# Attention weights left undivided, and the reciprocal of their sum applied to the attention output

## The chip, the core and the metric

The kernel runs on one core of a Trainium2 chip. The metric is device time in microseconds of one execution of the whole program, as the median of several runs; lower is better. Single rows come from one profiled execution, whose times are counted from its first instruction.

## The reference, cut to what matters

The program is one layer of a hybrid decoder: a sliding-window attention group and a state-space group side by side on 2064 tokens of a prompt (and 32 tokens of samples), an output projection, and a squared-ReLU MLP. The change touches the attention of the prompt only:

```python
def sink_softmax(logits, mask, sink):
    logits = jnp.where(mask, logits, NEG)
    m = jnp.maximum(jnp.max(logits, axis=-1, keepdims=True), sink)
    e = jnp.exp(logits - m)
    return e / (jnp.sum(e, axis=-1, keepdims=True) + jnp.exp(sink - m))

p = sink_softmax(logits, mask, sink)          # 8 heads, 2 key/value heads, window 128
o = jnp.einsum('bnkgqs,bnskd->bnqkgd', p, v)  # the output of a query is linear in its weights p
```

All arithmetic is float32. A product of two float32 tiles is made of three TensorE products of their high and low parts (helper `mm3`, L108; helper `split`, L93: ScalarE writes the rounded high part, and VectorE or GpSimd the difference).

## The kernel before

The program has four stages: a projection for the state-space input (`phase_u`), a loop over 16 tiles of 128 queries that carries attention and state space together (`phase_att`), the gated unit and output projection (`phase_mix`), and the MLP (`phase_mlp`). The order of instructions on each engine is fixed when the program is built: a planner walks the instructions in program order with its own estimate of when each is ready, so that neighbours in the code can be apart in a queue. Each engine then takes its queue strictly in order.

One turn of the loop at L993, for tile `i`:

- `scores` (L805): 24 products for two halves `u` (four heads each) into four banks of PSUM; VectorE adds the mask and takes the row maximum (L824); L827 forms minus the maximum of it and the sink; ScalarE makes the exponentials in `e` with their sums in `mx[:, u, 3]` (L830). L828 and L832 form the exponential of the sink's part in `mx[:, u, 2]`.
- `tr(i + 1)` (L781) turns the next tile's queries and keys; `qkv(i + 2)` (L431, L745) multiplies 48 products for the queries, keys and values of the tile after that, into two banks that `rope` reads.
- `rden` (L834): sum plus sink (L836), reciprocal (L837). `normal` (L839): the weights times the reciprocal, on VectorE for `u == 0` (L843, four instructions of 128x256) and on ScalarE for `u == 1` (L845, four).
- `ptrans` (L847): 16 transposes of `e` on TensorE (L852) into four banks, split by ScalarE into `PTh` and by VectorE into `PTl`.
- `rope(i + 2)` (L748): ScalarE takes queries, keys and values out of the two banks of `qkv` (L755, L754, L759); VectorE rotates them (L764 to L767) and reads the last of them at L768, which frees the second bank.
- `pv` (L858): 24 products of weights and values into one bank `po`; at the end of it ScalarE copies `po` into `at` with a change of column order (L871), and stores it in `ATD`.
- `split_x(i + 3)` (L735): ScalarE writes `axh`, GpSimd `axl` (L96).
- In between, one step of the state space (`s_split`, `s_in`, `s_rot`, `s_scan`, `s_hsplit`, `s_out`) and, on GpSimd, sums of MLP weights (L1476 to L1479).

Six banks of PSUM serve `scores`, `tr`, `qkv`, `ptrans` and `po` in turn (`mm_bank`, L75); a tile of the loop uses 13. Working tiles of 128x552 come from a pool of 25 (`t2`, L86), which the state space shares.

Of the kernel before, what the change touches and what calls it, by code (L numbers as in the profile page):

```python
# [58 lines left out]
def hymba_step(ctx: ExitStack, tc: tile.TileContext, A, O):  # L59
# [98 lines left out]

    # ------------------------------------------------------------------ u projection
    class Paced:  # L160
# [558 lines left out]
    def phase_att(outer, eq, qw, QP, X01):  # L719
        with ExitStack() as es:  # L720
# [6 lines left out]
            vr = [pw.tile([128, 4, 2, 192], F32R, name=f"v{n}") for n in range(2)]  # L727
            X, QK, QT, SM, PT, PO = {0: X01[0], 1: X01[1]}, {}, {}, {}, {}, {}

# [75 lines left out]
            def scores(i, u):  # L805
# [21 lines left out]
                DVE.scalar_tensor_tensor(mx[:, u, 1], mx[:, u, 0], -1.0, ng, op0=OP.mult, op1=OP.min)  # L827
                DVE.tensor_tensor(mx[:, u, 2], mx[:, u, 1], ng, op=OP.subtract)  # L828
                for j in range(4):
                    ACT.activation(e[:, u, j], e[:, u, j], AF.Exp, bias=mx[:, u, 1, j:j + 1],  # L830
                                   accum_out=mx[:, u, 3, j:j + 1])
                ACT.activation(mx[:, u, 2], mx[:, u, 2], AF.Exp)  # L832

            def rden(i, u):  # L834
                e, mx = SM[i]
                DVE.tensor_tensor(mx[:, u, 3], mx[:, u, 3], mx[:, u, 2], op=OP.add)  # L836
                DVE.reciprocal(mx[:, u, 3], mx[:, u, 3])  # L837

            def normal(i, u):  # L839
                e, mx = SM[i]  # L840
                for j in range(4):
                    if u == 0:
                        DVE.tensor_scalar(e[:, u, j], e[:, u, j], mx[:, u, 3, j:j + 1], None, op0=OP.mult)  # L843
                    else:
                        ACT.activation(e[:, u, j], e[:, u, j], AF.Copy, scale=mx[:, u, 3, j:j + 1])  # L845

# [11 lines left out]
            def pv(i, kv):  # L858
# [10 lines left out]
                if kv == 1:  # L869
                    at = wk.tile([128, 512], F32, name="at", tag="at", bufs=1)  # L870
                    ACT.activation(at.rearrange("p (k s c) -> p k c s", k=4, s=8),  # L871
                                   po.rearrange("p (k c s) -> p k c s", k=4, s=8), AF.Copy)
                    ACT.dma_start(ATD[:, :, :, 16 * i:16 * i + 16].rearrange("p k s c -> p (k s) c"),
                                  at.rearrange("p (a c) -> p a c", c=16))

            # state space: one pair of groups per step
            SX, SC, SS, SH = {}, {}, {}, {}
# [115 lines left out]
            for i in range(NT):  # L993
# [17 lines left out]
                for n, pr in enumerate(here):  # L1011
                    s_rot(pr)
                    if pr + 1 < NPR:
                        s_split(pr + 1)
                    if pr + 2 < NPR:
                        s_load(pr + 2)
                    if n == 0:
                        rden(i, 0)
                        normal(i, 0)
                        rden(i, 1)  # L1020
                        normal(i, 1)
                    s_scan(pr)
                    s_hsplit(pr)
                    if n == 0:
                        ptrans(i, 0)
                        if i + 2 < NT:
                            rope(i + 2)
                        ptrans(i, 1)
                    s_out(pr)
                    if pr + 1 < NPR:  # L1030
                        s_in(pr + 1)
                if not here:
                    for u in range(2):
                        rden(i, u)
                        normal(i, u)
                    ptrans(i, 0)
                    if i + 2 < NT:
                        rope(i + 2)
                    ptrans(i, 1)
                pv(i, 0)  # L1040
                if i + 3 < NT:
# [21 lines left out]

    # ------------------------------------------------------------------ gated unit, sample attention, output projection
    def advance(gen, n=1):
# [105 lines left out]
    def squares(pl, x, p, parts):  # L1171
        """sums of squares over the four channel tiles: [channel, token]"""
        q = pl.tile([128, 4, 128], F32, name="pq", tag="pq", bufs=1)
# [225 lines left out]

    # ------------------------------------------------------------------ MLP  # L1400
    # Both products are cut in halves along tokens, contraction and result (Strassen-Winograd): seven products
    # of quarters each, with the sums of the activations' quarters formed in place and those of the weights' once.
    HN = (336, 352, 352)
# [84 lines left out]
    def phase_mlp(pre):  # L1488
        with ExitStack() as es:
# [8 lines left out]
            def combine(p, n, pt, q, both):  # L1498
                """C11 = P1 + P2, C12 = P1 + P6 + P5 + P3, C21 = P1 + P6 + P7 - P4, C22 = P1 + P6 + P7 + P5"""
                if p == 1:  # L1500
# [47 lines left out]
            def rows(c, p):  # L1548
                """runs of up to 128 columns that hold tokens of one kind: (first column, number, rows of the output)"""
                out = []  # L1550
# [48 lines left out]
            def end_a(c, n):  # L1599
                """the first half of the features of the last tokens, scaled by the gain"""  # L1600
                f = M["H"].rearrange("p a c -> p (a c)")
# [171 lines left out]
```

## Time and profile before

| | us |
|---|---|
| median of 3 runs | 2208.49 |
| lowest and highest run | 2202.45, 2210.93 |
| the profiled execution, first to last instruction (its span) | 2198.8 |
| what the median has beside that span | 9.7 |
| the loop over 16 tiles, mean distance of its stages (from 211 to 564) | 23.6 |

The page gives no other time of the profiled execution than its span. Its first section has the busy time of each engine; the second cuts the span into 40 slices, with the share of each engine in tenths and the clock that TensorE was granted; the fourth follows the work that ended last back from the end. A group of instructions is shown with its line, engine, output and input, shape, count, busy time, mean duration, and the idle time of the engine in front of it with what ended that idle time. Matmuls overlap, and the ends of their rows are modelled, so that a duration there is longer than the distance to the next.

### The profile page before, as it was taken

Reading aid. Unit: us, or ns where it says so; the run is one execution under the profiler, and the core shown is the slowest. Engines: PE = TensorE matmul, PEld = TensorE weight load, DVE = VectorE, ACT = ScalarE, POOL = GpSimd, SP = SyncE. Lnnn points to the kernel's source line nnn. Section 1 sums busy time; section 2 is a strip of 40 time slices with the busy share of each in tenths; the row PEclk is TensorE's granted clock in tenths of the full one; section 3 lists DMA queues with packets and bytes.
Section 4 is the critical chain, followed back from the end, with each engine's and each line's share of the span. In section 5 each row is a group of like instructions: output and inputs, shape, how many; then the busy total and the mean of one; then the engine's idle time right before and its main releaser. Section 6 shows DMA issues by size and latency. Waiting matters only on the chain.

```text
span 2198.8 us, 37175 instructions
## 1 busy us (share of the span) xinstructions
PE 2083.1 (95%) x12968; PEld 1963.3 (89%) x12968; DVE 1645.6 (75%) x3412; ACT 1324.0 (60%) x2877; POOL 397.2 (18%) x435
## 2 busy tenths in 40 slices
PE   7888999997799999989999999999999999999997
PEld 7877888786678787889999999999999999999995
DVE  8947788788678647469896885787868757787686
ACT  6644655555665545537865555588555555875555
POOL 5513545455142334000000000000000000000001
PEclk9998999998899999999999999999999999999999
DMA  8894666655577526778745465454454564444554
GB/s 291 240 222 117 158 183 169 166 155 158 168 224 256 184 85 209 221 240 287 246 144 144 136 189 184 139 191 135 137 143 149 176 181 138 158 135 140 134 161 151
DMA packets 351972, 387.16 MB, mean 176 GB/s; under 512 B 96504, under 2 KB 239512, under 8 KB 351768
## 3 DMA queue, kind: packets, MB, share of 16 engines
q1 hardware_dynamic: 285096, 378.13, 56.9%
q10 hardware_dynamic: 65792, 4.20, 1.8%
q0 software_dynamic: 896, 2.46, 0.4%
q8 instruction: 101, 1.65, 0.3%
q14 instruction: 87, 0.71, 0.1%
HBM read 303.26 MB, written 82.46 MB: 175 GB/s over the span
## 4 chain that ended last, share of the span: by engine, by line
PE 70%; DVE 10%; DMA 9%; ACT 4%; issue 4%; POOL 1%; SPq 1%; POOLq 0%; DVEq 0%; ACTq 0%
PE mm L111 20%; PE mm L110 20%; PE mm L112 20%; PE mm L436 2%; PE mm L819 2%; DMA Y<-in_w_down_dram 2%; PE mm L437 1%; DMA wr<-TU 1%; DVE e L843 1%; DMA zu<-YD 1%; DMA wt<-in_w_down_dram 1%; DVE wsl L96 1%; DVE e L824 1%; DMA qwr<-in_w_in_dram 1%; ACT e L845 1%
## 5 line engine op out<-in xcount | busy, mean ns | idle before, releaser
L111 PE MATMUL mm<-vl,wsh 128*128 128x352 f32 (+1 forms) x2624 | 839.9, 320 | 0.0
L110 PE MATMUL mm<-vh,wsh 128*128 128x352 f32 (+1 forms) x2624 | 839.3, 321 | 0.1
L112 PE MATMUL mm<-vh,wsl 128*128 128x352 f32 (+1 forms) x2624 | 816.4, 321 | 12.1 <-DVE wsl L96 11.9
L95 ACT ACTIVATE wsh<-wr 128x512 fp32r<-128x512 f32 x684 | 430.3, 629 | 440.0 <-PE mm L111 425.5
L96 DVE TENSOR_TENSOR wsl<-wr,wsh 128x512 fp32r<-128x512 f32 x684 | 471.4, 691 | 178.4 <-ACT wsh L95 177.4
L112 PEld LDWEIGHTS mm<-vh,wsl 128*128 128x128 f32 x2624 | 489.2, 188 | 15.5 <-DVE wsl L96 15.4
L110 PEld LDWEIGHTS mm<-vh,wsh 128*128 128x128 f32 x2624 | 494.6, 189 | 0.6 <-ACT wsh L95 0.4
L111 PEld LDWEIGHTS mm<-vl,wsh 128*128 128x128 f32 x2624 | 494.1, 188 | 0.0
L154 POOL TENSOR_TENSOR yst<-yst,nhalf 128x1 f32<-128x1 f32 (+2 forms) x15 | 13.4, 896 | 1250.1 <-DVE yst L153 1250.1
L1496 DVE TENSOR_TENSOR U<-U,mm 128x352 f32<-128x352 f32 (+3 forms) x240 | 140.1, 584 | 74.0 <-PE mm L112 73.4
L96 DVE TENSOR_TENSOR vl<-U,vh 128x352 fp32r<-128x352 f32 (+3 forms) x348 | 175.9, 507 | 1.6 <-ACT vh L95 1.0
L95 ACT ACTIVATE vh<-U 128x352 fp32r<-128x352 f32 (+3 forms) x348 | 162.9, 470 | 6.1 <-PE mm L111 5.9
L1529 ACT ACTIVATE U<-U 128x352 f32<-128x352 f32 (+1 forms) x192 | 92.9, 485 | 24.0 <-DVE U L1496 19.8
L1530 ACT ACTIVATE U<-U 128x352 f32<-128x352 f32 (+1 forms) x192 | 93.8, 490 | 4.4
L110 PE MATMUL mm<-xh,uwh 128*128 128x264 f32 (+1 forms) x256 | 73.4, 297 | 12.9 <-DVE U L528 7.0
L830 ACT ACTIVATE e<-e,mx 128x256 f32<-128x256 f32 x128 | 63.3, 498 | 33.0 <-DVE mx L827 32.7
L436 PE MATMUL mm<-qw,axh 128*128 128x512 f32 x224 | 78.9, 399 | 0.0
L111 PE MATMUL mm<-xl,uwh 128*128 128x264 f32 (+1 forms) x256 | 75.2, 297 | 0.0
L112 PE MATMUL mm<-xh,uwl 128*128 128x264 f32 (+1 forms) x256 | 73.0, 295 | 0.0
L764 DVE TENSOR_TENSOR ra<-qk,cs 128x160 f32<-128x160 f32 (+1 forms) x17 | 22.6, 1331 | 54.5 <-ACT qk L754 54.4
L819 PE MATMUL mm<-kT,qTh 64*128 64x256 f32 x256 | 54.4, 323 | 9.1 <-DVE v L768 9.1
L110 PEld LDWEIGHTS mm<-xh,uwh 128*128 128x128 f32 x256 | 50.1, 199 | 13.6 <-DVE U L528 7.5
(417 smaller groups left out, 4012.4 us busy)
## 6 DMA issues: line engine op xcount, KB each, us to landing
wr<-TU SPq DMA_DIRECT2D x192, 256.0 KB
wr<-TD SPq DMA_DIRECT2D x192, 256.0 KB
wr<-in_w_down_dram SPq DMA_DIRECT2D x156, 256.0 KB
wr<-in_w_up_dram SPq DMA_DIRECT2D x144, 256.0 KB
wt<-in_w_up_dram SPq DMA_DIRECT2D x32, 512.0 KB
TU<-wt SPq DMA_DIRECT2D x32, 512.0 KB
Y<-in_w_down_dram SPq DMA_DIRECT2D x20, 512.0 KB
TD<-Y SPq DMA_DIRECT2D x20, 512.0 KB
```

The costliest lines, as they stand in the source:

```text
L95: ACT.activation(hi, src, AF.Copy)
L96: (eng or DVE).tensor_tensor(lo, src, r(hi), op=OP.subtract)
L110: PE.matmul(out, ah, bh, start=start, stop=False)
L111: PE.matmul(out, ah, bl, start=False, stop=False)
L112: LAST[0] = PE.matmul(out, al, bh, start=False, stop=stop)
L436: PE.matmul(pq[:n], lh(k), rh[k][:, 0:512], start=st, stop=sp_)
L764: DVE.tensor_tensor(a[:n], t[:n, :, 0:16], c, op=OP.mult)
L819: PE.matmul(pts[kv][:, 256 * p:256 * p + 256], q, kTr[ki][sl, a:b + 1:b - a, :], start=(x == 0), stop=(x == 2))
L830: ACT.activation(e[:, u, j], e[:, u, j], AF.Exp, bias=mx[:, u, 1, j:j + 1], accum_out=mx[:, u, 3, j:j + 1])
L1496: DVE.tensor_tensor(out, a, b, op=OP.add)
L1529: ACT.activation(x, x, AF.Relu)
L1530: ACT.activation(x, x, AF.Square)
```

## The change

The weights stay the bare exponentials. `normal` is gone. `rden` is done once for a tile, for both halves: the sink's exponent (one subtraction and one ScalarE exponential of 8 columns), the sum and the reciprocal. A new `rows_of` spreads the 8 reciprocals of a query over 64 columns each (ScalarE, 128x512), turns that on TensorE with four transposes into one more bank of PSUM, and has ScalarE copy it out, so that it has one column for each query and one partition for each output channel. The copy of `po` becomes a VectorE multiplication of `po` with that tile, whose output is written in order and whose two inputs are read with a step of 8 columns. The new tiles `rb` and `rc` come from the pool of 25.

```diff
@@ scores
                 DVE.scalar_tensor_tensor(mx[:, u, 1], mx[:, u, 0], -1.0, ng, op0=OP.mult, op1=OP.min)
-                DVE.tensor_tensor(mx[:, u, 2], mx[:, u, 1], ng, op=OP.subtract)
...
-                ACT.activation(mx[:, u, 2], mx[:, u, 2], AF.Exp)
-
-            def rden(i, u):
-                e, mx = SM[i]
-                DVE.tensor_tensor(mx[:, u, 3], mx[:, u, 3], mx[:, u, 2], op=OP.add)
-                DVE.reciprocal(mx[:, u, 3], mx[:, u, 3])
-
-            def normal(i, u):
-                e, mx = SM[i]
+
+            def rden(i):
+                mx = SM[i][1]
+                DVE.tensor_tensor(mx[:, :, 2], mx[:, :, 1], negsink.rearrange("p (j u) -> p u j", u=2), op=OP.subtract)
+                ACT.activation(mx[:, :, 2], mx[:, :, 2], AF.Exp)
+                DVE.tensor_tensor(mx[:, :, 3], mx[:, :, 3], mx[:, :, 2], op=OP.add)
+                DVE.reciprocal(mx[:, :, 3], mx[:, :, 3])
+
+            def rows_of(i):
+                mx = SM[i][1]
+                pb = mm_bank()
+                rb = t2("rb", [512])
+                ACT.activation(rb.rearrange("p (j u d) -> p j u d", j=4, u=2),
+                               mx[:, :, 3].rearrange("p u j -> p j u")[:, :, :, None].to_broadcast([128, 4, 2, 64]), AF.Copy)
                 for j in range(4):
-                    if u == 0:
-                        DVE.tensor_scalar(e[:, u, j], e[:, u, j], mx[:, u, 3, j:j + 1], None, op0=OP.mult)
-                    else:
-                        ACT.activation(e[:, u, j], e[:, u, j], AF.Copy, scale=mx[:, u, 3, j:j + 1])
+                    PE.transpose(pb[:, 128 * j:128 * j + 128], rb[:, 128 * j:128 * j + 128], ident)
+                rb = t2("rc", [512])
+                ACT.activation(rb, pb, AF.Copy)
+                return rb
@@ pv
-                    ACT.activation(at.rearrange("p (k s c) -> p k c s", k=4, s=8),
-                                   po.rearrange("p (k c s) -> p k c s", k=4, s=8), AF.Copy)
+                    DVE.tensor_tensor(at.rearrange("p (k s c) -> p k s c", k=4, s=8),
+                                      po.rearrange("p (k c s) -> p k s c", k=4, s=8),
+                                      RB[i].rearrange("p (k c s) -> p k s c", k=4, s=8), op=OP.mult)
@@ the loop, with a step of the state space (and the same without one)
                     if n == 0:
-                        rden(i, 0)
-                        normal(i, 0)
-                        rden(i, 1)
-                        normal(i, 1)
+                        rden(i)
                     s_scan(pr)
                     s_hsplit(pr)
                     if n == 0:
                         ptrans(i, 0)
                         if i + 2 < NT:
                             rope(i + 2)
                         ptrans(i, 1)
+                        RB[i] = rows_of(i)
                     s_out(pr)
```

## Rows read from the trace of the kernel before

**Rows 1.** The profile page, its first line: the span.

```profile
span 2198.8 us, 37175 instructions
```

**Rows 2.** Stages, `at` to `at`: length; PE, PEld, DVE, ACT, POOL busy; clock, DMA, GB/s.

```profile
307.30:329.69 22.39, 21.98 (x150) 18.73 (x149) 19.49 (x46) 13.93 (x41) 12.54 (x13) 1.00 0.62 165
...
375.66:404.32 28.66, 25.91 (x146) 22.04 (x144) 22.00 (x53) 16.23 (x49) 15.66 (x17) 0.82 0.66 174
```

**Rows 3.** The chain that ended last, 180 to 570 us, shares by line.

```profile
by line: PE mm L819 11.0%; PE mm L436 10.8%; issue 7.0%; PE mm L437 5.8%; DVE e L843 4.9%; PE mm L111 3.8%; DVE e L824 3.6%; ACT e L845 3.5%; PE b L110 2.8%; DVE sg L931 2.7%; PE mm L112 2.3%; PE mm L110 2.3%; DVE hst L939 2.2%; ACT axh L95
```

**Rows 4.** The same chain piece by piece, in one tile: start, duration, work.

```profile
311.93 3.02 DVE e L843 x4
...
317.04 0.95 ACT axh L95
```

**Rows 5.** Waits of the loop, 180 to 570 us: us in total, times, longest.

```profile
DVE ra L764 <- ACT qk L754: 47.2, 14, 5.4
ACT e L845 <- DVE mx L837: 32.4, 15, 4.0
ACT wz L95 <- DMA sb<-BD: 28.5, 6, 6.5
...
PE mm L819 <- DVE v L768: 9.1, 8, 2.0
```

**Rows 6.** End of `qkv` on PE and start of L755 on ACT: first, one middle, last tile.

```profile
192.53 0.28 PE L437 MATMUL mm<-qw,axl 128*128 128x256 f32 x1
...
193.47 0.67 ACT L755 ACTIVATE qk<-mm,rq 128x512 f32<-128x512 f32 x1
...
315.74 0.28 PE L437 MATMUL mm<-qw,axl 128*128 128x256 f32 x1
...
317.89 0.67 ACT L755 ACTIVATE qk<-mm,rq 128x512 f32<-128x512 f32 x1
...
506.98 0.28 PE L437 MATMUL mm<-qw,axl 128*128 128x256 f32 x1
...
507.48 0.67 ACT L755 ACTIVATE qk<-mm,rq 128x512 f32<-128x512 f32 x1
```

**Rows 7.** Groups by line and shape, 180 to 570 us: busy us, mean ns, idle before.

```profile
L843 DVE TENSOR_SCALAR e<-e,mx 128x256 f32<-128x256 f32 x64 | 32.5, 567 | 0.4
L845 ACT ACTIVATE e<-e,mx 128x256 f32<-128x256 f32 x64 | 27.3, 497 | 32.4 <-DVE mx L837 32.4
L871 ACT ACTIVATE at<-mm 128x512 f32<-128x512 f32 x16 | 17.0, 1062 | 11.8 <-PE mm L112 11.7
L95 ACT ACTIVATE PTh<-mm 128x512 fp32r<-128x512 f32 x64 | 34.3, 613 | 0.6 <-PE mm L852 0.6
L96 DVE TENSOR_TENSOR PTl<-mm,PTh 128x512 fp32r<-128x512 f32 x64 | 40.8, 677 | 5.2 <-ACT PTh L95 5.2
L96 DVE TENSOR_TENSOR kT<-mm,kT 128x128 fp32r<-128x128 f32 x15 | 4.2, 278 | 2.1 <-ACT kT L95 2.1
```

**Rows 8.** L843 and L764 in the whole span, ns least/median/most.

```profile
L843 DVE TENSOR_SCALAR e<-e,mx x64: 337/467/899, 187.9 to 554.3; 128x256 f32<-128x256 f32 x64
...
L764 DVE TENSOR_TENSOR ra<-qk,cs x17: 307/1747/1807, 163.3 to 508.4; 128x160 f32<-128x160 f32 x16, 48x160 f32<-48x160 f32 x1
```

**Rows 9.** GpSimd and VectorE in order of time behind 318 us.

```profile
318.06 2.36 POOL L96 TENSOR_TENSOR axl<-axr,axh 128x1024 fp32r<-128x1024 f32 x1 [3.26 <-ACT axh L95]
...
318.84 1.76 DVE L764 TENSOR_TENSOR ra<-qk,cs 128x160 f32<-128x160 f32 x1 [2.79 <-ACT qk L754]
```

**Rows 10.** TensorE: four transposes of 128x128 and what follows them.

```profile
307.08 0.60 PE L788 MATMUL mm<-ident,qk 128*128 128x128 f32 x4
307.43 0.48 PE L436 MATMUL mm<-qw,axh 128*128 128x512 f32 x1
```

**Rows 11.** A VectorE multiplication of PSUM that changes column order, 27 to 123 us.

```profile
L528 DVE TENSOR_TENSOR U<-mm,rr x28: 599/646/692, 27.1 to 122.6; 128x264 f32<-128x264 f32 x28
```

**Rows 12.** The chain at the end of the loop: start, duration, work.

```profile
555.04 1.71 ACT e L845 x4
```

More of the change, by code (lines that the diff above doesn't have):

```diff
@@ L727, in phase_att @@
             vr = [pw.tile([128, 4, 2, 192], F32R, name=f"v{n}") for n in range(2)]
-            X, QK, QT, SM, PT, PO = {0: X01[0], 1: X01[1]}, {}, {}, {}, {}, {}
+            X, QK, QT, SM, PT, PO, RB = {0: X01[0], 1: X01[1]}, {}, {}, {}, {}, {}, {}
             def load_x(i):
@@ L1032, in phase_att @@
                 if not here:
-                    for u in range(2):
-                        rden(i, u)
-                        normal(i, u)
+                    rden(i)
                     ptrans(i, 0)
@@ L1039, in phase_att @@
                     ptrans(i, 1)
+                    RB[i] = rows_of(i)
                 pv(i, 0)
```

## The prediction

> **What bounds the kernel now.** I read the span first, 2198.8 us [rows 1]; the median of the runs, 2208.49, is 9.7 us more, and I keep that difference. Only the loop over the 16 tiles issues other work after the change, so the question is what sets the length of a tile there. The windows from one `at` copy to the next answer half of it: a quick tile takes 22.4 us and its TensorE row is full (21.98 busy), at the full clock; a slow one takes 28.7 us at a granted clock of 0.82 [rows 2]. Fifteen such stages average 23.6 us. So TensorE is never far from being the bound, but something holds it from time to time.
>
> The chain that ended last says what: of 390 us in the loop, L843 has 4.9% and L845 3.5%, that is 19.1 and 13.7 us [rows 3]. Piece by piece, in one tile, they stand in a row: VectorE scales half of the weights (3.02 us from 311.93), ScalarE then has the other half, and only at 317.04 writes `axh`, behind which it takes the queries out of PSUM [rows 4]. The waits show both ends of that: ScalarE stands still in front of L845 for 32.4 us in all until VectorE has the second reciprocal, VectorE in front of L764 for 47.2 us until ScalarE has taken `qk` out, and TensorE's next scores wait for L768, the instruction that gives back the second bank of `qkv` [rows 5]. The reader is to see a loop of three engines: reciprocal, scaling, ScalarE's queue, `rope`, a bank, scores.
>
> How much of that is slack? `qk` can't be taken out before `qkv` has ended on TensorE. The last `qkv` product ends at 316.02 and L755 starts at 317.89, so 1.9 us could go in this tile; in the first tile it is 0.7, in the last 0.2 [rows 6]. Over the 14 tiles the gaps are 0.7, 0.7, 2.6, 0.9, 3.4, 1.9, 2.3, 1.6, 3.2, 0.5, 4.0, 1.9, 0.4 and 0.2: 24.1 us in sum. The smallest, 0.2, is what a handover takes, so 24.1 - 14 x 0.2 = **21 us** can go before `qkv` itself is what is late.
>
> **The change part by part.** *Weights not scaled.* This takes 32.5 us of VectorE and 27.3 us of ScalarE out of the loop [rows 7], and the reciprocal out of the path to the transposes. The path gains the 21 us above, not the 33 us of the chain: what is late next is the end of `qkv`. That `axh`, which stands between L845 and L755, moves forward needs no new cover: ScalarE stood idle in front of L845 for 32.4 / 15 = 2.2 us a tile [rows 5], and `axh` takes 0.95 [rows 4].
>
> *A second-order gain: GpSimd and VectorE.* One L843 took 337 ns at best and 567 on average [rows 7, 8], and L764 took 307 ns at best but 1747 as a median [rows 8]. In the tile shown L764 starts at 318.84, while GpSimd's `axl` runs from 318.06 to 320.42, and ends 0.2 us behind it [rows 9]. `axl` follows `axh`; if `axh` comes about 3 us earlier, `axl` is over before L764. At most 12 long L764 give back 1.44 us each, 17 us. I take half, 8 us, since in some tiles `axh` will still be late.
> The Trainium skill, SBUF — State Buffer, section Who interferes with whom, says that VectorE and GpSimd share a pair of ports as an exclusive lock, and that the second to come is blocked to the end of the other's instruction. Rows 9 agree in the end times; by this rule the whole 17 us would be free wherever the two no longer overlap.
>
> *Clock.* The stage at 0.82 granted 28.66 x 0.18 = 5.2 us less than the full clock [rows 2], behind a stretch where TensorE stood. With shorter waits some of it returns: from 0 to 5.2, taken at 3.
>
> *End of the loop.* Behind the last tile the chain has L845 for 1.71 us [rows 12]; 2 us go with the reciprocal in front of it.
>
> *Small operations.* Two subtractions, sums, reciprocals and ScalarE exponentials of 4 columns become one each of 8. None is priced: they lie inside the waits that go.
>
> *Spreading and turning.* Four transposes take 307.43 - 307.08 = 0.35 us [rows 10], 16 x 0.35 = 5.6 us of TensorE. Behind `qkv` TensorE waits for L768 anyway in half of the tiles (8 waits [rows 5]), so half is hidden: +3. The two ScalarE copies are priced at 0.61 us each, by the PSUM copy of the same size [rows 7]. The first lies in the idle time in front of `axh`; if that cover is gone it costs 10 us. The second is queued among `PTh` copies that `pv` waits for: 0 to 0.61 a tile, taken at 0.25, x 14 = +3.5.
>
> *The multiplication.* L871 leaves ScalarE (1.06 us a tile) and VectorE gets 512 columns with a step in both inputs. From below: the subtraction of the same shape without a step, 0.677 us. From above: L528, the same kind of multiplication with changed order, takes 0.646 us for 264 columns; without a step a column costs (677 - 278) / 384 = 1.04 ns, and 264 would take 0.42, so the step costs 0.23, and twice that for 512 columns: 1.12 us [rows 7, 11]. I take 1.1, since L528 is the nearer row. It comes behind `pv`, while TensorE runs the 8.6 us of `qkv`; in the tile shown VectorE is done with its part of that stretch when it finishes L843, 3 us of which go. So it costs nothing on the path. If it were all on it: 16 x 1.12 = 18 us.
> The store of `at` stays on ScalarE's queue, and now waits there for VectorE; the next exponentials queue behind it. Up to now ScalarE waited 11.7 us for `pv` at this place and copied for 17.0 [rows 7]; so the new wait can give back 17 us of ScalarE's time or add the 18 of the multiplication. I take 0: both end at about the same moment.
> The Trainium skill, Advanced Engine Details and Errata, section Memory Cachelines, speaks against this part: lines are 16 bytes in SBUF and 8 in PSUM, and an access to another line each time is slower, with no figure. A step of 8 columns is 32 bytes, so each element is on another line. No run of this case shows a stepped read; L528 has its step on the written side.
>
> *The added wait and bank.* `rows_of` takes a 14th bank of PSUM in a tile, in program order in front of `po` and of the next scores; until ScalarE's copy is out the next user of that bank waits. TensorE's queue is in order, so behind the four transposes stand `s_in` and `pv`, and they wait for ScalarE's spread and so for the reciprocal. From below this is nothing. From above it is the wait that L845 has now, 32.4 us. The nearest row is TensorE's wait for L768's bank, 9.1 us; I take half of that, +4, as the reciprocal comes 3 us earlier than now.
> The pool of 25 tiles gives two more a turn to `rb` and `rc`. A load of the state space that has to wait for one is issued later on SP's queue, with the weight loads behind it. The loop now has 28.5 us of ScalarE's waits for `sb` [rows 5]; the price lies between nothing and as much again. Loads run a tile ahead, so I stay near the lower end: +2.
>
> Sum on the profiled execution: -21 - 8 - 3 - 2 + 3 + 3.5 + 4 + 2 = -21.5 us, 2198.8 to 2177.3; on the median, 2208.5 to **2187 us**.
>
> **The rivals.** *TensorE full in every tile (deeper).* The lock between GpSimd and VectorE is gone everywhere, the clock stays full, and the added operations all hide but the transposes: -21 - 17 - 5 - 2 + 5.6 = -39, 2169 us. For it speaks that quick tiles already have a full TensorE row; against it, that the full row of the quick tile still contains 1.9 us of slack, so other fine waits will show.
>
> *Eaten up (same).* The gain of 21 is there, but VectorE is the next bound: the multiplication comes on the path in every tile (+18) and half of the transposes too (+3). 2208.5 us. VectorE is busy 19.5 of 22.4 us in the quick tile [rows 2], which speaks for it; that 2.3 us of L843 leave for 1.1 that come speaks against it.
>
> *The wait moves to TensorE (slower).* The place is the four new transposes in TensorE's queue. If the planner puts them right behind `qkv` while VectorE, held by GpSimd, gives the reciprocal as late as now, the 32.4 us of L845's wait stand on TensorE, with 5.6 of transposes: -21 + 32.4 + 5.6 = +17, 2225 us. It decides from a wait of (21 - 5.6) / 16 = about 1 us a tile upwards. Against it: the first reciprocal is there by 311.93, when L843 starts [rows 4], and `qkv` runs to 316.02 [rows 6], 4 us in which the one reciprocal that is left and the spread can be done.
>
> **How the numbers follow.** I give the forecast 0.55, the deeper case 0.2, eaten up 0.14 and slower 0.11. A measurement of this kernel tells apart about 0.5%, so 2197.4 and 2219.5 are the bounds. Faster holds the forecast and the deeper case, and a little of eaten up: 0.76; same 0.14; slower 0.10. The range goes from somewhat below the deeper case, 2163, to 2207, 20 us above the forecast: the multiplication, or the loads, or the bank may cost that, one of them but not all. Most of eaten up and all of slower stay outside.
>
> **What would show each step.** Right: L755 starts within 0.5 us of the end of `qkv` in all tiles; L764 no longer waits 47 us, and its median falls from 1.75 us; ScalarE's row has no wait for L837 of that size; the multiplication takes 1.0 to 1.2 us. Wrong: TensorE waits for the spread or its copy, or scores wait for the 14th bank; VectorE's multiplication has a wait for `pv` with L936 and the exponentials of the next half queued behind it. The forecast fails if the planner's new order puts the spread in front of `qk` with its reciprocal still late, or if the fine waits between `PTl` and the scores, which this change leaves alone, grow by what the `qk` path gives.

## The result and the profile after

The changed kernel takes 2215.97 us (median of 9 runs, 2211.74 to 2226.61); the kernel before took 2205.95 us beside it (9 runs). The ratio is 1.0059, with a 95% interval of 1.0042 to 1.0076: slower by 0.6%, where 2187 us was forecast, and outside the range. The profiled execution has a span of 2213.3 us, 14.5 more than [rows 1]. All ratios here leave out one disturbed execution, 5132 us, of experiment e2.

The loop has less to do than before, yet its tiles are longer. L755, once a tile, gives their length. First the kernel before, sixth tile (the last one, 507.48, stands in [rows 6]); then the changed kernel, the same tile and the last (in the rows ACT is ScalarE, DVE VectorE, POOL GpSimd, PE TensorE and PEld its weight loads):

```profile
270.23 0.67 ACT L755 ACTIVATE qk<-mm,rq 128x512 f32<-128x512 f32 x1
```

```profile
280.69 0.67 ACT L755 ACTIVATE qk<-mm,rq 128x512 f32<-128x512 f32 x1
...
532.62 0.67 ACT L755 ACTIVATE qk<-mm,rq 128x512 f32<-128x512 f32 x1
```

Ten tiles took (507.48 - 270.23) / 10 = 23.7 us each before, and (532.62 - 280.69) / 10 = 25.2 now: 1.5 us more a tile, 14.7 in ten, about the 14.5 of the span. This is a mean: from this tile on the changed kernel's tiles alternate between 24.2 us and 27.1 to 27.3 until near the end of the loop, and both kinds belong to the argument below. The 10.5 us that the changed kernel is late by in the first of these tiles come back: from its last L755 to the end it takes 1680.7 us, the kernel before 1691.3. The likely reason is that up to its last L755 it has written 14 results of the state space, the kernel before 13, so that one pair less is left. The rows group the copies of these results out of PSUM, before and after:

```profile
L960 ACT ACTIVATE sy<-b x13: 592/612/638, 181.0 to 486.6; 128x536 f32<-128x536 f32 x13
```

```profile
L967 ACT ACTIVATE sy<-b x14: 622/672/676, 196.8 to 513.0; 128x536 f32<-128x536 f32 x14
```

What is dearer in a tile shows in one window over the steady part, 300 to 480 us (length; PE, PEld, DVE, ACT, POOL busy; granted clock, DMA share, GB/s), before and after:

```profile
300.00:480.00 180.00, 171.63 (x1100) 146.91 (x1100) 149.56 (x397) 103.58 (x287) 94.20 (x97) 0.95 0.63 167
```

```profile
300.00:480.00 180.00, 168.24 (x1042) 144.71 (x1041) 134.27 (x328) 89.73 (x245) 88.24 (x92) 0.89 0.58 157
```

VectorE and ScalarE are less busy, as they should be. TensorE stands a little more (11.8 us of 180 against 8.4), and its granted clock is 0.89 instead of 0.95. What it waits for in the same 180 us, before and after:

```profile
PE mm L110 <- ACT PTh L95: 3.6, 3, 1.7
PE mm L819 <- DVE v L768: 3.5, 3, 1.2
```

```profile
PE mm L110 <- DVE v L768: 9.2, 7, 1.7
```

The waits of the loop, 180 to 570 us, as in [rows 5] (total, times, longest):

```profile
ACT e L829 <- DVE mx L827: 120.7, 28, 6.2
...
ACT wz L95 <- DMA sb<-BD: 8.1, 2, 7.6
...
ACT rb L845 <- DVE mx L838: 4.6, 11, 0.5
...
DVE sz L927 <- PE b L112: 27.6, 11, 4.0
DVE ra L764 <- ACT qk L754: 19.6, 14, 3.7
```

The waits of [rows 5] did shrink: L764's from 47.2 to 19.6, the loads' from 28.5 to 8.1, and the spread `rb` waits only 4.6 us for its reciprocal. In their place VectorE waits 27.6 us for the input products of the state space (L927), which is new, and the exponentials (L829) wait 120.7 us for their maximum, where they waited 32.7 before. That last number is no measure of the loss: in e4 below it is 95.3, and e4 is faster than both kernels.

One turn between two tiles, at the start of a 27.1-us tile, shows why. ScalarE, start, duration, work:

```profile
406.33 0.63 ACT L845 ACTIVATE rb<-mx 128x512 f32<-128x512 f32 x1 [0.34 <-DVE mx L838]
406.86 1.04 ACT L95 ACTIVATE axh<-axr 128x1024 fp32r<-128x1024 f32 x1
407.81 0.67 ACT L755 ACTIVATE qk<-mm,rq 128x512 f32<-128x512 f32 x1
...
408.88 2.06 ACT L95 ACTIVATE PTh<-mm 128x512 fp32r<-128x512 f32 x4
410.79 0.64 ACT L850 ACTIVATE rc<-mm 128x512 f32<-128x512 f32 x1
411.27 0.67 ACT L967 ACTIVATE sy<-b 128x536 f32<-128x536 f32 x1
```

TensorE in the same turn (L437 ends `qkv`, L964 the state-space result, `b` from `wz` are the input products):

```profile
404.76 0.28 PE L437 MATMUL mm<-qw,axl 128*128 128x256 f32 x1
...
409.12 0.39 PE L964 MATMUL b<-shh,ctl 64*128 64x268 f32 x1
411.23 0.55 PE L110 MATMUL mm<-PTh,v 128*128 128x256 f32 x1 [1.73 <-DVE v L768]
...
419.08 0.60 PE L110 MATMUL b<-sxh,wz 128*128 128x276 f32 x1
419.48 0.43 PE L111 MATMUL b<-sxl,wz 128*128 128x276 f32 x1
419.71 0.43 PE L112 MATMUL b<-sxh,wz 128*128 128x276 f32 x1
...
421.52 0.29 PE L111 MATMUL b<-sxl,wz 128*128 128x276 f32 x1
421.65 0.28 PE L112 MATMUL b<-sxh,wz 128*128 128x276 f32 x1
421.77 0.28 PE L111 MATMUL mm<-PTl,v 128*128 128x256 f32 x1
```

And VectorE, to which the input products go:

```profile
422.03 0.70 DVE L927 TENSOR_TENSOR sz<-b,se 128x516 f32<-128x516 f32 x1 [3.95 <-PE b L112]
...
424.67 1.22 DVE L877 TENSOR_TENSOR at<-mm,rc 128x512 f32<-128x512 f32 x1
425.74 0.48 DVE L824 CUSTOM_DVE_ANT_0 e<-mm,masks 128x256 f32<-128x256 f32 x1
```

The result and the input products of the state space share the only pair of banks of the tag `b2`. The result is complete at 409.5, but ScalarE copies it (L967) last of all, behind four copies of `PTh` and that of the rows, so the pair is free at 411.9. Until the rope has given back a bank (L768) TensorE has nothing: 1.73 us. From there its products stand 0.21 to 0.23 us apart (419.48 to 419.71), where products of that size stand 0.12 to 0.13 apart at the full clock (421.52 to 421.65), and this lasts to 421.3: the half level, 1.2 GHz. The input products come at 419.1, behind 19 of the 24 scores. VectorE waits 3.95 us for them, and its second set of maxima comes late, and so do the exponentials. The turn of the next tile has the same order on ScalarE, but the gap at that place is 0.79 us and the products stay 0.12 to 0.13 us apart. From 300 to 480 us the two kinds of turn alternate: four of the gaps last 1.73 to 1.74 us, each with some 10 us at the half level, and three 0.75 to 0.79 without.

In the kernel before, one turn of that kind was full. ScalarE's result copy and what follows, then TensorE:

```profile
318.96 0.61 ACT L960 ACTIVATE sy<-b 128x536 f32<-128x536 f32 x1
319.46 2.06 ACT L95 ACTIVATE PTh<-mm 128x512 fp32r<-128x512 f32 x4
```

```profile
319.62 0.39 PE L110 MATMUL b<-sxh,wz 128*128 128x276 f32 x1 [0.41 <-ACT sy L960]
...
321.25 0.28 PE L110 MATMUL mm<-PTh,v 128*128 128x256 f32 x1
```

There the result was copied ahead of the four `PTh`, and the twelve input products ran from 319.6 to 321.25, just in the time that the rope takes. Not every turn before was like this: around 295, 389 and 441 us the copy stands behind one or two `PTh`, TensorE has gaps of 1.5 to 1.75 us, and some of the half level follows; hence its 0.95.

### The profile page after: what moved, and what is told of

Same layout as the page of the kernel before. It is cut to its first block, busy times and chain, and to the rows that moved or that the text cites. A ratio compares the mean times of both kernels' runs of the same rounds, so it can differ in the third digit from the quotient of the medians.

```text
span 2213.3 us, 37193 instructions
## 1 busy us (share of the span) xinstructions
PE 2081.7 (94%) x13032; PEld 1962.4 (89%) x13032; DVE 1639.4 (74%) x3316; ACT 1304.5 (59%) x2813; POOL 399.0 (18%) x435
## 4 chain that ended last, share of the span: by engine, by line
PE 70%; DVE 11%; DMA 9%; ACT 4%; issue 4%; POOL 1%; SPq 0%; DVEq 0%; POOLq 0%; ACTq 0%
PE mm L111 21%; PE mm L110 20%; PE mm L112 20%; DMA Y<-in_w_down_dram 3%; PE mm L819 2%; PE mm L436 2%; DMA wt<-in_w_down_dram 1%; DMA xr<-in_xT_dram 1%; PE mm L437 1%; DVE sg L938 1%; PE b L110 1%; DVE e L824 1%; PE b L1574 1%; DVE sz L931 1%; DMA zu<-YD 1%
## 5 line engine op out<-in xcount | busy, mean ns | idle before, releaser
L112 PE MATMUL mm<-vh,wsl 128*128 128x352 f32 (+1 forms) x2624 | 815.5, 321 | 14.7 <-DVE wsl L96 14.6
L829 ACT ACTIVATE e<-e,mx 128x256 f32<-128x256 f32 x128 | 63.7, 500 | 122.2 <-DVE mx L827 122.2
L110 PE MATMUL mm<-oh,psh 128*128 128x512 f32 (+1 forms) x136 | 56.8, 418 | 6.1 <-ACT zt L1122 4.0
L824 DVE CUSTOM_DVE_ANT_0 e<-mm,masks 128x256 f32<-128x256 f32 x128 | 47.4, 422 | 17.8 <-PE mm L819 17.8
```

Source lines behind the costliest of these rows:

```text
L110: PE.matmul(out, ah, bh, start=start, stop=False)
L112: LAST[0] = PE.matmul(out, al, bh, start=False, stop=stop)
L824: DVE.tensor_tensor_reduce(e[:, u, j], pts[kv][:, 256 * p:256 * p + 256], masks[m], 1.0, -3e38, op0=OP.add, op1=OP.max, accum_out=mx[:, u, ...
```

## Experiments

Ratios are to the kernel before on the same chip, with their 95% intervals. The kernel before took 2199.5 to 2201.6 us in these sets, less than the 2205.95 above, so across sets the ratios are to be compared, not the microseconds. "Clock" is the granted clock from 300 to 480 us.

**e1. The removal alone.** From the kernel before:

```
-                        normal(i, 0)
...
-                        normal(i, 1)
...
```

> The kernel before with the division of the weights left out and nothing put in its place (the output of attention is not divided by the sums). It prices the removal alone. Theory ORDER (the rows of reciprocals make the planner put the state-space result and its copy behind the copies of PTh, so that the state-space input products slip behind the scores): nothing is added here, so the input products stand ahead of the scores as before, the loop loses the waits at L755, and the time is 2185 us, 2170 to 2198. Theory MULTIPLICATION (the 1.2-us multiplication on VectorE's path is what costs): the same, 2185. Theory NOTHING TO GAIN (the removal itself is worth nothing, since VectorE and ScalarE only wait elsewhere): 2200 to 2210.

2200.5 us, ratio 1.0001 (0.9987 to 1.0016): NOTHING TO GAIN. The removal is worth nothing. Yet it did what the prediction wanted of it: the 14 gaps between the end of `qkv` and L755 fell from 24.1 us in sum to 8.4. TensorE, in 300 to 480 us, then waits for L768 in every one of seven tiles, and the clock is 0.92:

```profile
PE mm L819 <- DVE v L768: 8.6, 7, 1.9
```

```profile
300.00:480.00 180.00, 170.97 (x1074) 148.10 (x1074) 136.67 (x364) 94.31 (x259) 92.36 (x97) 0.92 0.60 159
```

**e2. The multiplication without the rows.** From the changed kernel:

```
-                                      RB[i].rearrange("p (k c s) -> p k s c", k=4, s=8), op=OP.mult)
+                                      cs[:, :16].rearrange("p t n d -> p (t n d)").rearrange("p (k c s) -> p k s c", k=4, s=8), op=OP.mult)
...
-                        RB[i] = rows_of(i)
...
```

> The changed kernel without the rows of reciprocals: no spread, no transposes, no copy from PSUM; VectorE still multiplies each tile's attention output as it leaves PSUM, in the same stepped form, by a table that lies in SBUF since before the loop (the cosines and sines; the result is not the attention output). Theory ORDER: the input products of the state space stand ahead of the scores again, and the time is that of the kernel without division plus at most 5 us, some 2185 to 2192. Theory MULTIPLICATION: 14 to 16 tiles pay 1.2 us each on VectorE's path, the time is some 18 us above the kernel without division and within 6 us of the changed one, 2205 to 2216.

2187.0 us, 0.9929 (0.9909 to 0.9950), clock 0.97. The multiplication doesn't make the changed kernel slow: with it alone the kernel is 0.7% faster than before. ORDER had it level with e1 or 5 us above; it is 0.7% below. What it has and e1 has not is, besides one sum and reciprocal for a tile instead of two, that `at` has left ScalarE, where in e1 the copy waits 35.1 us for `pv` (180 to 580 us) with the copies of `kT` and `qTh` and the exponentials behind it. That this wait is what makes e1 slower than e2 is not shown: in e10 below the copy waits still longer, 45.9 us, and e10 is the fastest of all. The line is from e1:

```profile
ACT at L871 <- PE mm L112: 35.1, 14, 11.3
```

**e3. The rows without the multiplication.** From the changed kernel:

```
-                    DVE.tensor_tensor(at.rearrange("p (k s c) -> p k s c", k=4, s=8),
...
+                    ACT.activation(at.rearrange("p (k s c) -> p k c s", k=4, s=8),
+                                   po.rearrange("p (k c s) -> p k c s", k=4, s=8), AF.Copy)
```

> The changed kernel with its rows of reciprocals made but not used: ScalarE copies the attention output from PSUM as in the kernel before (the output is not divided). VectorE has no multiplication. Theory ORDER: the static order still has the input products of the state space behind the scores, so the time stays with the changed kernel, 2208 to 2218. Theory MULTIPLICATION: VectorE's path is 16 x 1.2 us shorter, some 2197, 2190 to 2202.

2226.2 us, 1.0115 (1.0094 to 1.0135), clock 0.88. Slower still, and above both ranges: the loss comes with the rows, by what they cost or by what they do to the order.

**e4. The state space written first.** From the changed kernel, with nothing left out:

```
-                        ptrans(i, 1)
-                        RB[i] = rows_of(i)
                     s_out(pr)
                     if pr + 1 < NPR:
                         s_in(pr + 1)
+                    if n == 0:
+                        ptrans(i, 1)
+                        RB[i] = rows_of(i)
```

> The changed kernel, whole, with the state-space result of this step and the input products of the next written ahead of the second half of the weights' transposes and of the rows of reciprocals. Theory ORDER: the input products fill TensorE's wait for the rope again, VectorE's wait of 27.6 us for them is gone, and at least 10 of the changed kernel's us come back: 2190 to 2205. Theory MULTIPLICATION and a theory ADDED WORK (the spread, the transposes and the copy cost by themselves in the queues): nothing comes back, 2212 to 2220.

2182.6 us, 0.9915 (0.9898 to 0.9931), lower than expected. All operations of the change are there, the rows too, and 1.44% of the time, some 32 us, are gone against the changed kernel. So the loss was one of order. What the rows cost by themselves in this order was not measured: e2, without them, is at 0.9929, but its order is the planner's own. One turn, ScalarE and TensorE, and the window:

```profile
374.66 1.07 ACT L95 ACTIVATE PTh<-mm 128x512 fp32r<-128x512 f32 x2
375.61 0.62 ACT L967 ACTIVATE sy<-b 128x536 f32<-128x536 f32 x1
376.11 0.64 ACT L845 ACTIVATE rb<-mx 128x512 f32<-128x512 f32 x1
376.63 1.10 ACT L95 ACTIVATE PTh<-mm 128x512 fp32r<-128x512 f32 x2
```

```profile
376.29 0.40 PE L110 MATMUL b<-sxh,wz 128*128 128x276 f32 x1 [0.66 <-ACT sy L967]
...
377.91 0.60 PE L848 MATMUL mm<-ident,rb 128*128 128x128 f32 x4
```

```profile
300.00:480.00 180.00, 173.86 (x1230) 150.37 (x1229) 160.78 (x383) 100.71 (x280) 113.42 (x109) 1.00 0.70 181
```

The result is copied behind two `PTh`, not five copies; the input products fill the turn again, the gap is 0.66 us, and the clock stays at the full level. The twelve products take 1.62 us here and 2.69 in the turn of the changed kernel shown above. A tile takes 21.8 us, (502.92 - 285.02) / 10 by L755. Against the 25.2 of the changed kernel that is 3.4 us: TensorE is busy 21.05 us of a mean tile instead of 23.55 (its row's share times the tile), which the clock of 1.00 for 0.89 explains, and stands 0.74 instead of 1.65.

**e5. Input products forced ahead of the scores.** From the changed kernel:

```
+                            if "si" in LAST:
+                                pace(y, LAST.pop("si"))
...
                 SS[pr] = pS
+                LAST["si"] = LAST[0]
```

> The changed kernel, whole, with one constraint more: the state-space input products of the next step must stand ahead of the next tile's scores on TensorE. The copies of PTh, of the reciprocals' rows and of the state-space result keep their order on ScalarE. Theory INPUT PRODUCTS (that they slipped behind the scores is by itself what costs): VectorE's wait for them is gone and the time comes down to that of the run with the state space written first, 2180 to 2192. Theory SCALARE'S QUEUE (the state-space result is copied behind four copies of PTh and one of the rows, so its banks come free late, wherever the input products stand): TensorE now waits for those banks with the scores queued behind, and the time stays at 2203 to 2216.

2221.7 us, 1.0095 (1.0074 to 1.0115), clock 0.90. Slower than the changed kernel, and above both ranges. Where the input products stand is not what costs; this also contradicts the first part of the ORDER theory as e1 to e4 stated it. In one turn the result is copied until 389.7 and the input products start at 391.8, behind ten products of the weights; VectorE still waits for them (42.8 us from 180 to 570). TensorE's turn has two waits now, of 1.5 and 2.0 us a tile (300 to 480 us):

```profile
PE mm L110 <- DVE v L768: 14.3, 7, 2.0
PE mm L850 <- ACT qk L755: 10.8, 7, 2.0
```

**e6. `at` on VectorE in the kernel before.**

```
-                    ACT.activation(at.rearrange("p (k s c) -> p k c s", k=4, s=8),
...
+                    DVE.tensor_copy(at.rearrange("p (k s c) -> p k s c", k=4, s=8),
+                                    po.rearrange("p (k c s) -> p k s c", k=4, s=8))
```

> The kernel before, whole, with its division kept, but the attention output copied from PSUM by VectorE instead of ScalarE, in the stepped form of the multiplication. Theory AT (what the change can gain is that this copy no longer waits for the products on ScalarE with the copies of kT, qTh and the exponentials queued behind it; the division itself is worth nothing): 2183 to 2193, some 13 us below the kernel before, as between the run without division and the run with the multiplication only. Theory BOTH (the copy can only be moved for a gain when VectorE and ScalarE are rid of the division): 2196 to 2206.

2209.0 us, 1.0047 (1.0028 to 1.0065). Neither theory had this: with the division kept, the copy on VectorE costs 0.5%. The removal is worth nothing alone (e1) and the move less than nothing alone; both together gain 0.7% (e2).

**e7. The state space first in the kernel before.** The edit of e4 there (without the rows):

```
-                        ptrans(i, 1)
...
+                    if n == 0:
+                        ptrans(i, 1)
```

> The kernel before, whole, with the same lines moved as in the run with the state space written first (result of this step and input products of the next ahead of the second half of the weights' transposes). Theory ORDER (the move only undoes what the rows of reciprocals did to the order): nothing to undo here, 2194 to 2205. Theory BETTER ANYWHERE (that order is worth some 17 to 30 us to any of these kernels, and the change itself would still be a loss beside it): 2165 to 2188.

2202.9 us, 1.0006 (0.9991 to 1.0021): nothing. So that order is not better in itself; in the changed kernel it undoes a harm that the kernel before has less of, if at all.

**e8. Only the rows later.** From the changed kernel:

```
                         ptrans(i, 1)
-                        RB[i] = rows_of(i)
                     s_out(pr)
                     if pr + 1 < NPR:
                         s_in(pr + 1)
+                    if n == 0:
+                        RB[i] = rows_of(i)
```

> The changed kernel, whole, with only the rows of reciprocals written later: behind the state-space result of this step and the input products of the next, while both halves of the weights' transposes stay ahead of them. Theory ROWS FIRST (it is the rows, written ahead of the state space, that push it back): 2180 to 2193, as with the state space written first. Theory HALVES (the second half of the transposes and its copies must come behind the state space too, since the division no longer holds them back): 2203 to 2216.

2217.7 us, 1.0078 (1.0062 to 1.0095), clock 0.91: the theory of the halves, a little above its range. The rows are out of the way, the input products stand in the turn, but the result is still copied behind four `PTh`, and TensorE waits for its banks with all else behind. One turn: products of 276 columns at the half level (0.23 us apart), and at the end two of 256 at the full (0.12). It is one of the longer stretches; in most turns of e8 it is about half as long:

```profile
360.64 0.60 PE L110 MATMUL b<-sxh,wz 128*128 128x276 f32 x1 [2.81 <-ACT sy L967]
361.03 0.43 PE L111 MATMUL b<-sxl,wz 128*128 128x276 f32 x1
361.26 0.43 PE L112 MATMUL b<-sxh,wz 128*128 128x276 f32 x1
...
366.86 0.28 PE L111 MATMUL mm<-PTl,v 128*128 128x256 f32 x1
366.98 0.28 PE L112 MATMUL mm<-PTh,v 128*128 128x256 f32 x1
```

**e9. The result copied late, all else as in e4.** From e4 (`s_store` is the copy and store of `s_out`, now a function of its own):

```
+                x = ACT.activation(y, py[:, :, :NCY], AF.Copy, scale=0.25)
+                if "pt" in LAST:
+                    pace(x, LAST.pop("pt"))
...
+                    py = s_out(pr)
+                    if n == 0:
+                        ptrans(i, 1)
+                    s_store(pr, py)
```

> The version with the state space written first, with one thing taken back: on ScalarE the copy of the state-space result must stand behind the four copies of PTh (its products on TensorE stay where they were, between the two halves of the transposes). Theory COPY (this copy frees the only pair of banks that the input products can write; late, TensorE waits 2.5 to 3 us a tile for it with everything else behind, and its clock is at the half level after that): the wait for sy is back, the granted clock of 300 to 480 us falls from 1.00 to about 0.91, and the time is 2208 to 2222. Theory TRANSPOSES (what matters is only that the second half of the transposes no longer stands ahead of the state-space products on TensorE): 2180 to 2192.

2207.4 us, 1.0027 (1.0016 to 1.0038), clock 0.93, just under the low end of the COPY theory. Of the 1.44% between e4 and the changed kernel, 1.12 come back with this one constraint, eight tenths. The wait is there, 2.6 us a tile (300 to 480 us):

```profile
PE b L110 <- ACT sy L971: 21.0, 8, 2.8
```

Here and in e8 the input products stand ahead of the weights' products and scores, and TensorE waits at them; in the changed kernel they have slipped behind, and it waits for L768's bank. The late copy is common to all three. The planner also placed all 24 scores behind the products with the weights here, so it is the constraint with what the planner makes of it that was measured.

**e10. The state space first, `at` on ScalarE.** From e4, with the edit of e3.

> The version with the state space written first, with the multiplication left out: ScalarE copies the attention output from PSUM, so it is not divided; the rows are made and not used. TensorE's order is the same. It prices the multiplication where nothing else is out of order. Theory FREE (1.15 us a tile on VectorE lie beside TensorE's work, and on ScalarE the copy would hold back exponentials): the same time or later without it, 2181 to 2200. Theory MULTIPLICATION (it is on the path): 16 x 1.15 = 18 us less, 2163 to 2172.

2170.8 us, 0.9873 (0.9852 to 0.9894), clock 1.00, 21.1 us a tile, (485.55 - 274.36) / 10. Neither theory holds fully. Where nothing else is late the multiplication on VectorE does cost more than the copy on ScalarE: 0.42% or 9 us beside e4 (plus or minus 6, from the two intervals), half of the 18 that it takes in all. In the order of the changed kernel the same exchange went the other way: e3 against the changed kernel, 12 us.

**e11. The rows first.** From the changed kernel, with the lines of e4 moved and the rows ahead of `ptrans(i, 0)`:

```
+                        RB[i] = rows_of(i)
                         ptrans(i, 0)
```

> The changed kernel, whole, with the state-space result and input products written ahead of the second half of the transposes, and the rows of reciprocals ahead of both halves: the copy of the rows stands ahead of all copies of PTh, that of the state-space result behind two of these, the input products behind 12 of the 24 score products. Theory COPY: what counts is the copy of the state-space result; it is early, so the time is 2180 to 2195 although the input products come behind scores. Theory INPUT PRODUCTS (these have to stand ahead of the scores to fill TensorE's wait for the rope): TensorE has a gap of 2 to 3 us a tile again and the time is 2203 to 2218.

2185.5 us, 0.9938 (0.9922 to 0.9954), clock 0.99: the COPY theory. The input products come behind twelve scores here, which costs little if anything (e4 is 0.23% lower, about as much as the two intervals allow by chance); the result is copied behind two `PTh`, and TensorE's wait in the turn is small:

```profile
PE mm L819 <- DVE v L768: 5.2, 8, 0.7
```

**e12. The step of the multiplication on the written side.** From e4:

```
-                    DVE.tensor_tensor(at.rearrange("p (k s c) -> p k s c", k=4, s=8),
-                                      po.rearrange("p (k c s) -> p k s c", k=4, s=8),
-                                      RB[i].rearrange("p (k c s) -> p k s c", k=4, s=8), op=OP.mult)
+                    DVE.tensor_tensor(at.rearrange("p (k s c) -> p k c s", k=4, s=8),
+                                      po.rearrange("p (k c s) -> p k c s", k=4, s=8),
+                                      RB[i].rearrange("p (k c s) -> p k c s", k=4, s=8), op=OP.mult)
```

> The version with the state space written first, whole, with the multiplication in the other order of its loops: both operands are read in a row and the result is written in steps of 16 elements, where before both were read in steps of 8. All three engines keep their order. Theory STEPPED READ (the 1.15 us come from reading in steps): the multiplication takes 0.7 us as VectorE's other passes over 128x512 do, and of 16 x 0.45 = 7 us some two thirds are on the path, as 12 of its 18 us were when it was left out: 5 us below the version with the state space first, 2174 to 2181 where that has 2182.6. Theory ANY STEP: 1.1 to 1.2 us and the same time, 2180 to 2187.

2181.0 us, 0.9905 (0.9887 to 0.9923), not to be told from e4. The time lies at the edge of both ranges and decides nothing; the instruction does: 1.07 us, 7% less than in e4 and far from 0.7, so ANY STEP. The multiplication in e4 and in e12 (ns least/median/most):

```profile
L877 DVE TENSOR_TENSOR at<-mm,rc x16: 1097/1150/1178, 211.4 to 568.6; 128x512 f32<-128x512 f32 x16
```

```profile
L877 DVE TENSOR_TENSOR at<-mm,rc x16: 1037/1066/1084, 210.1 to 563.4; 128x512 f32<-128x512 f32 x16
```

e4, e11 and e12 compute all that the reference asks and beat both kernels: 0.85%, 0.62% and 0.95% below the kernel before.

## Why the prediction was wrong

**The step that failed** is the term of the added copies and banks. It asked whom the second ScalarE copy holds up, and named the `PTh` copies and `pv`, and of banks a 14th single one. It did not list what stands on ScalarE's queue behind them: the copy of the state-space result, which frees the only pair of banks that the input products can write. In the kernel before that copy stands behind none, one or two of the tile's `PTh` copies (none at 318.96); in the changed kernel it stands behind all four in every tile from 258 to 513 us, and behind the rows' copy. The term stood at 3.5 and 4 us; the order that it left out costs some 32 us against e4. That is the mean tile of 25.2 us, and e4, e8 and e9 take it apart: copy behind two 0.9915, behind four 1.0078 and 1.0027. In e3 and e5 too it stands behind four, at 1.0115 and 1.0095; in e10 and e11 behind two, at 0.9873 and 0.9938. e1 and e2 have no division either and don't lose: there the planner leaves `sy` behind two `PTh` copies at most. In e1 it stands at 318.07, 2.0 us behind that tile's L755, in the changed kernel 3.5 us behind (407.81 to 411.27). That it is the rows alone which make the planner put it last is not shown: in e8 they are written after it, and it is last all the same.

**The 21 us at L755** fail twice. The changed kernel doesn't have them: the spread and `axh` now stand between the exponentials and L755 (406.33 to 407.81 above), and the 14 gaps are 28.2 us in sum instead of 24.1. And they are worth nothing where they are had: in e1 the gaps are 8.4 and the time is the same, because TensorE waits for L768's bank all the same. "What is late next is the end of `qkv`" was the wrong next thing; it is what TensorE has to do between `qkv` and that bank. e4 comes out at the forecast's number (0.9915 of 2205.95 is 2187 us), but that is luck: of the 24.1 us of gaps 16.9 are still there, L764 is as long as before (1.77 us), and the gain is that of a clock at 1.00.

**The 8 us of the lock** did not come. L764 is as long as in [rows 8]:

```profile
L764 DVE TENSOR_TENSOR ra<-qk,cs x17: 324/1761/2487, 164.4 to 533.6; 128x160 f32<-128x160 f32 x16, 48x160 f32<-48x160 f32 x1
```

`axh` can't move ahead of the end of `qkv`, which reads the buffer that it writes (in e1 it waits 21.7 us for L437 in 12 tiles), so `axl` still runs where L764 starts (in the turn above from 407.98 to 410.34, L764 from 408.77 to 410.52). By the rule of the Trainium skill, SBUF — State Buffer, section Who interferes with whom, the second of the two engines waits for the first; these times and the median of 1.76 us beside 0.3 at best agree, and the error was in who would move.

**The clock** went the other way: 3 us were to be gained, and it fell from 0.95 to 0.89. It was taken as something that follows from the waits, and the 1.73-us gaps of the changed kernel agree; but this term was priced with fewer waits of TensorE, and they became more.

**The multiplication** was sized nearly right, 1.1 us against a median of 1.19 in the changed kernel, a little over the upper bound of 1.12. That it costs nothing on the path was wrong in the good order (9 of 18 us, e10) and too cautious in the planner's (e3 against the changed kernel, and e2 against e1). The prediction named the copy's wait for `pv` on ScalarE and took 0. That wait alone doesn't set the price: it is 35.1 us in e1 and 45.9 in e10, and only e10 is fast. The Trainium skill, Advanced Engine Details and Errata, section Memory Cachelines, expects an access that goes to another line each time to be slower; the stepped read agrees, 1.15 to 1.19 us beside the 0.677 of [rows 7] without a step. e12, whose reads are in a row and whose writes have a step of 16, takes 1.07, so a step on the written side costs nearly as much.

**Spread, turn, bank, loads.** `rb` took 0.63 us and its four transposes 0.35 (377.91 to 378.26 in e4), as priced. The bank's 4 us and the loads' 2 can't be priced from these runs: e4 with the rows is no slower than e2 without them, but the two differ in order as well. The loads' wait fell to 8.1 us.

**The rivals.** The sign was that of "the wait moves to TensorE", but not its mechanism: TensorE waits for the bank of L768, not for the reciprocal; the spread waited only 4.6 us for that. Its number, 2225, is the sum of a wait that did not come, so its nearness is luck. "Eaten up" (the multiplication on the path, no change) fell with e2.

**What stays open.** Why e1 gains nothing in the time although L755 is earlier is shown only as far as TensorE's wait for L768 and the clock of 0.92; why e2 is faster than e1, and why the copy on VectorE loses with the division kept (e6), was not taken apart. No run has the state space first without the rows. The half level was not separated from the gaps by a run that fills them with other work. They go together in the changed kernel, e4 and e8, but not everywhere: in e1 the full level stays after a gap of 1.85 us (344.49), and in e2 the half level comes from 429.8 on, behind a gap of only 0.63 us (427.14).

## What to carry to other kernels

Before pricing an edit, list for each engine what the edit lets go ahead of what, and who owns the banks that the overtaken instruction frees: a planner may put copies that are ready earlier ahead of a copy on which another engine's filler work hangs. What counted in this pipelined loop was whether TensorE had work in the one turn where it waits for the other engines; against e4 the changed kernel paid twice, 0.9 us a tile as idle time and 2.5 at the lower clock. And look at the new order of every engine's queue before giving a change up: here a few moved lines turned 0.6% slower into 0.85% faster.

## What the hardware showed

- A gap of TensorE of 1.73 us (changed kernel) or 2.81 us (e8) was followed by about 10 and 6 us at the half level, seen in products of the same size 0.23 us instead of 0.13 apart; in both cases the full level came back while TensorE was busy. After gaps of 0.66 us (e4) and 0.79 us (changed kernel) there was none. The length of the gap alone doesn't decide: there was none after 1.85 us in one turn of e1, and some 10 us after 0.63 us in one of e2.
- VectorE's multiplication of 128x512 from PSUM costs 1.07 us with the step on the written side and 1.15 with it on both read sides, where a pass without a step takes 0.68.
